# Decoder trunk: low parts of the input projections' weights and the rotary products on VectorE in place of GpSimd

## Chip, cores and metric

One core of one Trainium2 chip runs the whole program. The metric is the device time of one launch in microseconds (us). The kernel before took 2459.29 us, the median of three runs (2451.73 to 2461.47).

## What is computed

Two layers of a hybrid decoder on 1024 tokens of width 1024, in float32. Each layer has a mixer and a ConvFFN, each between two RMSNorms and added to the residual:

```python
h = rms_norm(x, norm_mix_pre[l])
proj = h @ w_in[l]                       # 1024 -> 3072, twelve slices of 256 columns
(c_a, c_gate, sb_q, sb_k, sb_v, r_q, r_k, r_v, r_g, sc_b, sc_c, sc_h) = jnp.split(proj, 12, axis=-1)
y_conf = conformer_conv(c_a, c_gate, ...)                  # depthwise conv of 31 taps, LayerNorm, SiLU
y_sb = stick_breaking_attention(sb_q, sb_k, sb_v)          # cumulative sums over keys
y_ret = retention_mixer(r_q, r_k, r_v, r_g, ...)           # rotary(q), rotary(k), chunks of 128
y_sc = short_gated_conv(sc_b, sc_c, sc_h, ...)             # 3 taps
mix = jnp.concatenate([y_conf, y_sb, y_ret, y_sc], -1) @ w_out[l]
x = x + rms_norm(mix, norm_mix_post[l])
f = conv_ffn(rms_norm(x, norm_ffn_pre[l]), ffn_up[l], ffn_conv_w[l], ffn_down[l])
x = x + rms_norm(f, norm_ffn_post[l])
```

`rotary` gives `x1*cos - x2*sin` and `x2*cos + x1*sin` for the two halves of each head of 64.

## The kernel before

**Split products.** A float32 matrix product is made of three products in the format fp32r: each operand is split into a high part (a cast, on ScalarE) and a low part (operand minus high part), and high*high, high*low and low*high are summed in PSUM. For the activations the parts are the resident tiles `hH` and `hL`; for the weights of the input projection they are `wh` and `wl`, made by `load_weight` (L189 to L196): a DMA of 512 KB into `wr` (L191), the cast `wh` on ScalarE (L193) and the subtraction `wl = wr - wh` (L195) on an engine that the caller names. There is one buffer `wr` and there are two of `wh` and `wl`: the next DMA into `wr` waits for L195, and a cast L193 waits until the projection two earlier has ended on TensorE.

**Projections.** `project` (L216) makes one block of 128 columns of the input projection in 8 steps, each of six matmuls of 512 columns (L210). There are 24 blocks in a layer (`IN_ORDER`). The list `WPOOL` names those whose L195 runs on GpSimd: 21 of the 24; `UPOOL` does so for the first six blocks of the up projection, which run the same way: one of six. So 44 subtractions L195 are on GpSimd (POOL in the profile) and 16 on VectorE (DVE).

**Order of the work.** Between the steps of the projections TensorE does the work of the attention groups, at slots set by hand: `run_slot` is called after each step, and inside the region `tc.manual_schedule` TensorE's order is as written. The other engines' orders are set when the program is built, by a scheduler with priorities and estimated costs; each engine then works strictly in that order and waits at semaphores.
- Stick-breaking attention, per unit: scores on TensorE into one PSUM tile (L361 to L364), three ACTIVATEs on ScalarE (L371 to L373), on VectorE a combination (L375) and a scan along the keys (L379), which reads the scores and so frees their tile for the next unit; then ScalarE (L381), transposes (L396), their split on ScalarE and VectorE (L181, L182), products with the values (L409) and their sums (L416 to L418).
- Conformer convolution: 31 taps for each of two channel blocks, each tap one operation of VectorE over 1023 columns or less with two inputs from SBUF (L261). They have a low priority and fill VectorE's order.
- Rotary products, `rotate` (L428 to L441): ScalarE copies the projected tile to SBUF, four DMAs swap the halves (L436), then `c = ps * c` on VectorE (L437) and on GpSimd `sw = sw * s` (L438) and `c = c + sw` (L439); the sum is split by L181 and L182. This is done for keys and queries of two head pairs, so 4 times in a layer.
- Retention: products per chunk on TensorE (L465 to L467), a chain of states over the chunks on VectorE and ScalarE (L474 to L479), scores (L490 to L492), their mask (L494), and outputs (L510, L512) with their sums (L514 to L516). L328, L329 split the queries of the second attention head pair; L314 are the value tiles' transposes; L524 takes a mean off in the retention's norm.

**Elsewhere.** `boundary` (L235) adds the residual and normalizes (L247, L249, L167); L731 is the output projection. The ConvFFN (L894 the products, L919 to L948 their evictions, L786 to L795 convolution and gate) and the down projection (L966, L967 the split, L977 the products) use GpSimd for L967. The first two weights of layer 2's input projection are loaded at the end of layer 1's ConvFFN.

Of the kernel before, what the change touches and what calls it, by code (L numbers as in the profile page):

```python
# [67 lines left out]
OTHER = (0, 2, 4)  # L68
HPR = 1000
HPW = 0  # L70
WPOOL = [0,1]+list(range(5,24))
UPOOL = (1,)
SKEW = 0
NPLAIN = 3
HPE = 60
# [11 lines left out]
def trunk_kernel(ctx, tc, x, w_in, w_out, w_up, w_down, params, gains, consts, rope, out):  # L87
    nc = tc.nc
# [25 lines left out]
    def ualloc(dt=F32, shape=(P, T)):  # L114
        s = free.pop(0)
        count[0] += 1
        t = big.tile(list(shape), dt, tag=f"u{s}", name=f"u{s}_{count[0]}")
        slot_of[id(t)] = (s, t)
        return t
# [81 lines left out]
    def prefetch(n=1):  # L201
        while queue and len(ready) < n:
            with tc.high_priority(offset=HPW):
                ready.append(load_weight(*queue.pop(0)))
# [224 lines left out]
    def rotate(ps, cs, done):  # L429
        c, s = cs  # L430
        e = ualloc()
        nc.scalar.copy(e, ps)
        sw = ualloc()
        for b in range(4):
            o = b ^ 1
            nc.sync.dma_start(sw[32 * b:32 * b + 32], e[32 * o:32 * o + 32])  # L436
        nc.vector.tensor_mul(c, ps, c)  # L437
        nc.gpsimd.tensor_mul(sw, sw, s)  # L438
        nc.gpsimd.tensor_add(c, c, sw)  # L439
        done(e, sw, s)  # L440
        return c  # L441

# [102 lines left out]
    nc.scalar.preload_act_table_set("natural_log_exp_and_others")  # L545
    queue += [(w_in[0, n], nc.gpsimd if n in WPOOL else nc.vector) for n in range(24)]
    hhs = []
# [24 lines left out]
    for l in range(DEPTH):  # L572
# [44 lines left out]
        def evict(kind, i, ps, cs):  # L617
# [24 lines left out]
            elif kind == "sv":  # L642
# [5 lines left out]
                for u in st["units"]:  # L648
                    u.update(v=v2, y=y[2 + i])
            elif kind == "rk":  # L650
                st["rk"] = rotate(ps, cs, later)
            elif kind == "rq":
                st["rq"] = rotate(ps, cs, later)
            elif kind == "rv":
                rv = ualloc()
# [118 lines left out]
        gd = dr.tile([NF, P, T], F32, name=f"gd{l}")  # L774
        queue += [(w_up[l, n], nc.gpsimd if n in UPOOL else nc.vector) for n in range(2 * NPLAIN)]
        prefetch(2)
# [279 lines left out]
        for ci, ch in enumerate(chunks):  # L1056
            final = ci == len(chunks) - 1
            if final:
                if not last:
                    queue += [(w_in[l + 1, n], nc.gpsimd if n in WPOOL else nc.vector) for n in range(24)]  # L1060
                    prefetch(2)
# [92 lines left out]
```

## Time and profile before

| | |
|---|---|
| median of three runs | 2459.29 us (2451.73 to 2461.47) |
| the profiled execution | 2450.47 us, its span 2448.7 us |
| TensorE (PE) busy | 2335.7 us, 95% |
| VectorE (DVE) busy | 1630.6 us, 67% |
| ScalarE (ACT) busy | 1093.6 us, 45% |
| GpSimd (POOL) busy | 391.3 us, 16% |
| granted TensorE clock, mean | 0.983 |

Times in rows are us from the start of the span. The span has these stages: the first norms to 50, mixer of layer 1 to about 540, its ConvFFN to about 1240, mixer of layer 2 to about 1760, its ConvFFN to the end. "Busy" is the time between the recorded start and end of an engine's instructions, whatever they did in it; bracketed text behind a row is the idle time of the engine before it and what ended it. A granted clock of 1.00 is TensorE's level of 2.4 GHz, 0.50 that of 1.2 GHz.

### The profile page before, as it was taken

How to read it: one execution, taken by the hardware profiler on the slowest of the kernel's cores; microseconds unless marked ns; L12 is line 12 of the kernel's file. 1: busy time of each engine (PE TensorE's matmuls, PEld its weight loads, DVE VectorE, ACT ScalarE, POOL GpSimd, SP SyncE). 2: the span in 40 equal slices, each digit the busy share in tenths (PEclk: the TensorE clock that was granted, in tenths of full speed). 3: DMA queues.
4: the chain of work that ended last, by engine and by line, in shares of the span. 5: the costliest groups of instructions: out<-in, count | busy, mean ns of one | idle time of the engine just before them, and what ended most of it. 6: DMA issues, size and time to landing. Idle time of an engine off the chain costs nothing. (4 is left out here: it accounts for less than half of the span.)

```text
span 2448.7 us, 26417 instructions
## 1 busy us (share of the span) xinstructions
PE 2335.7 (95%) x10596; PEld 1905.8 (78%) x10596; DVE 1630.6 (67%) x1657; ACT 1093.6 (45%) x1479; POOL 391.3 (16%) x160
## 2 busy tenths in 40 slices
PE   7988999999999999899999889999999999989998
PEld 6866787777888887688778667877788888877887
DVE  5599665649687777444556995656497787763445
ACT  5652564434454545511246435644344454553202
POOL 1131120000000002743111312100000000045520
PEclk9998999999999999999999989999999999999999
DMA  4212112312222223423222122123122222224213
GB/s 146 69 43 61 52 44 78 124 73 79 69 78 87 94 78 136 158 82 115 74 82 78 44 60 61 35 72 135 61 86 86 78 78 86 95 103 172 86 69 121
DMA packets 58811, 209.88 MB, mean 86 GB/s; under 512 B 7104, under 2 KB 7872, under 8 KB 58688
## 3 DMA queue, kind: packets, MB, share of 16 engines
q1 hardware_dynamic: 58688, 208.19, 25.3%
q8 instruction: 83, 1.36, 0.2%
q14 instruction: 40, 0.33, 0.0%
HBM read 159.93 MB, written 39.85 MB: 82 GB/s over the span
## 5 line engine op out<-in xcount | busy, mean ns | idle before, releaser
L261 DVE SCALAR_TENSOR_TENSOR u<-u,par,u 128x1023 f32<-128x1023 f32 (+11 forms) x280 | 393.4, 1417 | 46.3 <-ACT u L786 41.3
L989 DVE TENSOR_TENSOR u<-u,pp 128x1024 f32<-128x1024 f32 x143 | 174.6, 1221 | 238.1 <-PE pp L977 238.0
L210 PE MATMUL pp<-hH,wh 128*128 128x512 f32 x960 | 326.9, 411 | 0.6 <-DVE u L182 0.6
L210 PE MATMUL pp<-hL,wh 128*128 128x512 f32 x960 | 312.4, 396 | 0.0
L210 PE MATMUL pp<-hH,wl 128*128 128x512 f32 x960 | 310.5, 394 | 0.0
L977 PE MATMUL pp<-u,u 128*128 128x512 f32 x1152 | 271.7, 396 | 16.7 <-ACT u L948 9.6
L967 POOL TENSOR_TENSOR u<-u,u 128x1024 fp32r<-128x1024 f32 x48 | 120.0, 2517 | 1039.1 <-DVE u L940 956.7
L977 PEld LDWEIGHTS pp<-u,u 128*128 128x128 f32 x1152 | 218.5, 191 | 66.8 <-ACT u L948 10.4
L195 POOL TENSOR_TENSOR wl<-wr,wh 128x1024 fp32r<-128x1024 f32 x44 | 111.0, 2522 | 742.4 <-ACT wh L193 742.2
L210 PEld LDWEIGHTS pp<-hL,wh 128*128 128x128 f32 x960 | 183.3, 191 | 40.3
L210 PEld LDWEIGHTS pp<-hH,wl 128*128 128x128 f32 x960 | 182.7, 190 | 40.2
L210 PEld LDWEIGHTS pp<-hH,wh 128*128 128x128 f32 x960 | 172.4, 192 | 36.4 <-issue 4.8
L731 PE MATMUL pp<-u,hH 128*128 128x512 f32 x512 | 140.6, 395 | 0.5 <-ACT u L181 0.4
L977 PE MATMUL pp<-hH 128*128 128x512 f32 x576 | 131.5, 389 | 0.0
L977 PEld LDWEIGHTS pp<-hH 128*128 128x128 f32 x576 | 108.1, 188 | 22.5
L894 PE MATMUL ppx<-u,wh 128*128 128x512 f32 x384 | 118.6, 390 | 1.8 <-ACT u L935 1.5
L786 ACT ACTIVATE u<-u,par 128x1024 f32<-128x1024 f32 x76 | 87.7, 1154 | 71.2 <-DVE u L940 65.7
L731 PEld LDWEIGHTS pp<-u,hH 128*128 128x128 f32 x512 | 95.8, 190 | 21.0 <-ACT u L181 1.4
L966 ACT CAST u<-u 128x1024 fp32r<-128x1024 f32 x48 | 50.1, 1050 | 138.2 <-DMA u<-in_w_down 87.2
L894 PE MATMUL ppx<-u,hH 128*128 128x512 f32 x352 | 108.5, 389 | 1.5 <-ACT u L919 1.5
L193 ACT CAST wh<-wr 128x1024 fp32r<-128x1024 f32 x60 | 63.0, 1049 | 95.5 <-PE pp L210 55.1
L182 DVE TENSOR_TENSOR u<-tp,u 128x512 fp32r<-128x512 f32 x96 | 62.4, 683 | 38.9 <-ACT u L181 38.6
(244 smaller groups left out, 4550.5 us busy)
## 6 DMA issues: line engine op xcount, KB each, us to landing
wr<-in_w_up SPq DMA_DIRECT2D x50, 512.0 KB, 3.5
wr<-in_w_in SPq DMA_DIRECT2D x48, 512.0 KB, 3.6
gd<-u SPq DMA_DIRECT2D x44, 512.0 KB, 2.9
u<-in_w_down SPq DMA_DIRECT2D x44, 512.0 KB, 4.8
u<-gd SPq DMA_DIRECT2D x44, 512.0 KB, 4.2
u<-in_w_up SPq DMA_DIRECT2D x38, 512.0 KB, 4.2
xs<-u SPq DMA_DIRECT2D x24, 512.0 KB, 2.6
u<-xs SPq DMA_DIRECT2D x24, 512.0 KB, 3.5
```

What stands on the lines that cost most here:

```text
L182: nc.vector.tensor_sub(l, src, h.bitcast(F32))
L193: nc.scalar.copy(wh, raw)
L195: eng.tensor_sub(wl, raw, wh.bitcast(F32))
L210: nc.tensor.matmul(ps[:, half * 512:(half + 1) * 512], w[:, kt, :], m[:, 4 * half:4 * half + 4, kt, :], start=(kt == 0 and m is hH and w i ...
L261: eng.scalar_tensor_tensor(acc[:, lo:hi], src[:, lo - s:hi - s], wc, acc[:, lo:hi], ALU.mult, ALU.add)
L731: nc.tensor.matmul(ps[:, hs], a[:, t, k, :], w[:, hs], start=(k == 0 and a is hH and w is wo[k][0]), stop=(k == KT - 1 and a is hL))
L786: nc.scalar.activation(acc, ps, AF.Copy, scale=par[:, w + 2:w + 3])
L894: nc.tensor.matmul(ps, a[:, kt, :], x(m, kt), start=start and kt == 0 and a is wh and m == 0, stop=kt == 3 and a is wl, skip_group_check=True)
L966: nc.scalar.copy(h, raw)
L967: (nc.gpsimd if n is not None or len(slot_of) % 2 else nc.vector).tensor_sub(lo, raw, h.bitcast(F32))
L977: nc.tensor.matmul(ps[:, hs], a[:, ts_], w[:, hs], start=(i == 0 and w is h and a is gh), stop=(i == len(gs) - 1 and a is gl))
L989: nc.vector.tensor_add(facc[t], facc[t], ps)
```

## The change

```diff
-WPOOL = [0,1]+list(range(5,24))
-UPOOL = (1,)
+WPOOL = []
+UPOOL = ()
...
         nc.vector.tensor_mul(c, ps, c)
-        nc.gpsimd.tensor_mul(sw, sw, s)
-        nc.gpsimd.tensor_add(c, c, sw)
+        nc.vector.tensor_mul(sw, sw, s)
+        nc.vector.tensor_add(c, c, sw)
```

All 60 subtractions L195 and the 16 operations L438 and L439 are then in VectorE's order; nothing of what is computed changes. On GpSimd 60 operations fewer are left (L967 and L247 stay). The scheduler sets VectorE's order anew. In the rows below `-` is a row of before only and `+` one of the change only.

On VectorE, layer 1, around the scan L379 of the tile `pp_23` (`u_49` and `u_54` are the accumulators of the two convolutions, `u_64` and `u_55` the rotated key's swapped and direct parts, `u_83` its low part):

```order
+L261 SCALAR_TENSOR_TENSOR u_49_842<-u_48_839,par,u_49_842 128x1011
+L438 TENSOR_TENSOR u_64_1108<-u_64_1108,u_56_979 128x1024
 L182 TENSOR_TENSOR u_71_1214<-tp,u_71_1214 128x4x128
 L182 TENSOR_TENSOR u_72_1222<-tp,u_72_1222 128x4x128
 L375 SCALAR_TENSOR_TENSOR u_70_1202<-pp_23_1189,u_69_1198 128x1024
-L182 TENSOR_TENSOR u_83_1464<-u_55_977,u_82_1463 128x1024
+L439 TENSOR_TENSOR u_55_977<-u_55_977,u_64_1108 128x1024
 L379 SCALAR_TENSOR_TENSOR u_70_1202<-pp_23_1189,u_70_1202 128x383
 L379 SCALAR_TENSOR_TENSOR u_70_1202<-pp_23_1189,u_70_1202 128x639
 L437 TENSOR_TENSOR u_67_1133<-pp_22_1137,u_67_1133 128x1024
+L195 TENSOR_TENSOR wl<-wr,wh 128x1024
 L417 TENSOR_TENSOR u_27_487<-op,u_27_487 64x2x128
```

The two rotary operations stand in front of the scan now, the split of the key behind it, and a weight's low part between the scan and the sums L417, L418.

On VectorE, layer 1, where the retention's chain of states begins (L474; a tap's last number tells how far the convolution is, from 1023 down to 994):

```order
-L261 SCALAR_TENSOR_TENSOR u_54_975<-u_53_971,par,u_54_975 128x1012
-L261 SCALAR_TENSOR_TENSOR u_54_975<-u_53_971,par,u_54_975 128x1011
-L261 SCALAR_TENSOR_TENSOR u_54_975<-u_53_971,par,u_54_975 128x1010
 L474 COPY acc_1546<-pp_28_1548 64x64 x2
 L476 SCALAR_TENSOR_TENSOR acc_1547<-acc_1546,gam,pp_28_1548 64x64 x2
-L261 SCALAR_TENSOR_TENSOR u_54_975<-u_53_971,par,u_54_975 128x1009
 L479 SCALAR_TENSOR_TENSOR u_90_1545<-acc_1546,gam,u_90_1545 128x64
+L261 SCALAR_TENSOR_TENSOR u_49_842<-u_48_839,par,u_49_842 128x997
```

Before, 44 taps stand ahead of L474 (the first accumulator is done to 994, the second to 1010). With the change 35 do (to 998 and to 1015); the nine others are later in the order.

On VectorE, layer 1, the first unit of the second attention head pair, as it was:

```order
L261 SCALAR_TENSOR_TENSOR u_54_975<-u_53_971,par,u_54_975 128x994
L516 TENSOR_TENSOR u_95_1653<-pp_34_1792,u_95_1653 64x512
L375 SCALAR_TENSOR_TENSOR u_105_1814<-pp_35_1804,u_104_1810 128x1024
L379 SCALAR_TENSOR_TENSOR u_105_1814<-pp_35_1804,u_105_1814 128x1023
L515 TENSOR_TENSOR u_95_1653<-pp_36_1839,u_95_1653 64x512
L516 TENSOR_TENSOR u_95_1653<-pp_36_1839,u_95_1653 64x512
```

The last tap is done ahead of this scan, and nothing stands between L375 and L379. The same place with the change:

```order
L375 SCALAR_TENSOR_TENSOR u_105_1814<-pp_35_1804,u_104_1810 128x1024
L195 TENSOR_TENSOR wl<-wr,wh 128x1024
L379 SCALAR_TENSOR_TENSOR u_105_1814<-pp_35_1804,u_105_1814 128x1023
L261 SCALAR_TENSOR_TENSOR u_54_975<-u_53_971,par,u_54_975 128x1002
L261 SCALAR_TENSOR_TENSOR u_54_975<-u_53_971,par,u_54_975 128x1001
L261 SCALAR_TENSOR_TENSOR u_54_975<-u_53_971,par,u_54_975 128x1000
L515 TENSOR_TENSOR u_95_1653<-pp_36_1839,u_95_1653 64x512
```

A weight's low part stands between L375 and the scan, and late taps behind the scan.

## Rows read from the trace of the kernel before

**Rows 1.** Page, busy time of the engines (us, share of the span, instructions).
```profile
PE 2335.7 (95%) x10596; PEld 1905.8 (78%) x10596; DVE 1630.6 (67%) x1657; ACT 1093.6 (45%) x1479; POOL 391.3 (16%) x160
```

**Rows 2.** Stretches: length; PE, PEld, DVE, ACT, POOL busy (count); clock, DMA share, GB/s.
```profile
113.60:216.70 103.10, 89.34 (x434) 72.71 (x434) 101.64 (x90) 51.04 (x63) 26.02 (x10) 0.97 0.15 47
...
252.90:290.00 37.10, 36.01 (x150) 26.87 (x150) 18.86 (x22) 20.21 (x25) 4.77 (x2) 0.90 0.17 53
...
1332.40:1435.50 103.10, 89.31 (x434) 72.64 (x434) 101.68 (x90) 50.99 (x63) 26.98 (x10) 0.97 0.16 46
...
223.10:233.10 10.00, 8.25 (x31) 7.58 (x32) 9.77 (x14) 1.90 (x6) 0.00 (x0) 0.50 0.34 79
250.40:260.40 10.00, 9.81 (x22) 6.89 (x23) 5.31 (x7) 3.72 (x4) 0.00 (x0) 0.50 0.00 0
```

**Rows 3.** What TensorE waited for, 113.6 to 265: total us, times, longest.
```profile
PE pp L361 <- DVE u L379: 8.0, 4, 2.9
PE pp L490 <- DVE u L182: 5.6, 1, 5.6
PE op L409 <- DVE u L182: 3.1, 2, 3.0
...
PE tp L314 <- DVE u L182: 1.6, 1, 1.6
```

**Rows 4.** Groups by line: busy us, mean ns; first 113.6 to 216.7, then all.
```profile
L261 DVE SCALAR_TENSOR_TENSOR u<-u,par,u 128x1023 f32<-128x1023 f32 (+29 forms) x44 | 66.1, 1536 | 0.9 <-ACT u L268 0.4
...
L261 DVE SCALAR_TENSOR_TENSOR u<-u,par,u x280: 1235/1279/3431, 113.7 to 2204.5; 128x1023 f32<-128x1023 f32 x82, 128x1021 f32<-128x1021 f32 x4, 128x1019 f32<-128x1019 f32 x4, 128x1017 f32<-128x1017 f32 x4
...
L195 POOL TENSOR_TENSOR wl<-wr,wh 128x1024 fp32r<-128x1024 f32 x44 | 111.0, 2522 | 742.4 <-ACT wh L193 742.2
...
L439 POOL TENSOR_TENSOR u<-u,u 128x1024 f32<-128x1024 f32 x8 | 21.7, 2717 | 0.6
...
L195 DVE TENSOR_TENSOR wl<-wr,wh 128x1024 fp32r<-128x1024 f32 x16 | 19.5, 1220 | 31.3 <-ACT wh L193 31.3
```

**Rows 5.** Order of time, POOL and DVE: start us, length us, instruction [idle before].
```profile
142.11 2.65 POOL L195 TENSOR_TENSOR wl<-wr,wh 128x1024 fp32r<-128x1024 f32 x1 [17.29 <-ACT wh L193]
...
142.40 3.43 DVE L261 SCALAR_TENSOR_TENSOR u<-u,par,u 128x1022 f32<-128x1022 f32 x1
...
162.80 3.14 DVE L182 TENSOR_TENSOR u<-u,u 128x1024 fp32r<-128x1024 f32 x1
```

**Rows 6.** Order of time, end of the chunk products and what follows.
```profile
210.70 0.28 PE L467 MATMUL pp<-u,u 128*128 128x128 f32 x1
...
216.64 0.21 DVE L474 COPY acc<-pp 64x64 f32<-64x64 f32 x1
...
235.86 1.04 ACT L193 CAST wh<-wr 128x1024 fp32r<-128x1024 f32 x1 [2.34 <-issue]
```

**Rows 7.** Order of time, the scan of the second pair's first unit.
```profile
260.09 1.23 DVE L375 SCALAR_TENSOR_TENSOR u<-pp,u 128x1024 f32<-128x1024 f32 x1 [2.17 <-ACT u L373]
261.35 2.35 DVE L379 TENSOR_TENSOR_SCAN u<-pp,u 128x1023 f32<-128x1023 f32 x1
...
262.38 1.05 ACT L193 CAST wh<-wr 128x1024 fp32r<-128x1024 f32 x1 [2.33 <-PE pp L210]
...
263.84 0.36 PE L510 MATMUL pp<-u,u 128*128 128x256 f32 x1 [1.09 <-DVE u L379]
```

**Rows 8.** Order of time, other places where a DVE instruction is long.
```profile
17.60 3.39 DVE L167 SCALAR_TENSOR_TENSOR u<-u,r,u 128x1024 f32<-128x1024 f32 x1
...
473.16 3.41 DVE L249 SCALAR_TENSOR_TENSOR u<-u,r,u 128x1024 f32<-128x1024 f32 x1 [2.56 <-ACT r L158]
...
473.10 2.39 POOL L195 TENSOR_TENSOR wl<-wr,wh 128x1024 fp32r<-128x1024 f32 x1 [61.75 <-ACT wh L193]
...
960.96 3.31 DVE L261 SCALAR_TENSOR_TENSOR u<-u,par,u 128x1022 f32<-128x1022 f32 x1
...
965.89 0.50 PE L894 MATMUL ppx<-u,hH 128*128 128x512 f32 x1 [1.48 <-ACT u L919]
```

## The prediction
> **What bounds the kernel now.** I read the page first. TensorE is busy for 95% of the span and VectorE for 67% [rows 1], so by the means TensorE is the bound and VectorE has room. The table of stretches says otherwise for one stage. From 113.6 to 216.7, where the first attention head pair, the convolutions and the rotary products meet, VectorE is busy for 101.64 of 103.10 us and TensorE for 89.34; layer 2 has the same stretch at 1332.4 with the same figures [rows 2]. So there TensorE idles 13.8 us in each layer, and the table of its waits says for what: for the scan L379 8.0 us, for the splits L182 ahead of L409 3.1 and of L314 1.6; behind the stretch another 5.6 for the split that L490 needs [rows 3]. All of it waits for VectorE. In this stage VectorE is the bound, and a microsecond taken from its work ahead of such a gate is worth about one.
>
> Then the question is what VectorE does with its 101.64 us. The groups show 44 taps L261 there, at 1536 ns, where the median of all 280 is 1279 and the longest 3431 [rows 4]. In order of time the reason shows: a tap that starts at 142.40, inside a subtraction on GpSimd from 142.11 to 144.76, takes 3.43 us and ends 1.07 after it; a split L182 at 162.80 takes 3.14 [rows 5], where an operation of that shape takes 1.22 [rows 4]. Such an operation, with both inputs in SBUF, stands still while GpSimd works and is then done; the trace books the wait as busy. So GpSimd's work is not free here: in the stretch it costs VectorE 44 x (1536 - 1279) ns = 11.3 us at the taps and 3.14 - 1.22 = 1.9 at that split, 13.2 in all.
>
> **The change part by part.**
>
> *The stretch ahead of L474, in both layers.* It gains the 13.2 us. It takes on five of the L195 and four of the rotary operations: 9 x 1.22 = 11.0 us. And nine taps leave it (44 to 35 in the second piece of the order), 9 x 1.28 = 11.5. Net: 13.2 + 11.5 - 11.0 = 13.7 us less ahead of L474. L474 is late now: its chunk products end at 210.98, it starts at 216.64 [rows 6], and the 5.6 us at L490 are this delay handed on. I don't take the whole 13.7. The first piece of the order shows two gates with added work ahead of them: L439 ahead of the scan, L195 ahead of L418. What stands behind them on ScalarE comes later by that, and VectorE meets it. I leave out two operations, 2.4 us: **-11.3 us a layer**. Bounds: -13.7, if no gate binds; 0, if what VectorE loses to GpSimd is time in which it would have waited anyway (its idle time there is 1.5 us, which speaks against that).
>
> *From L474 to the second pair.* One L195 stands there behind the chain's operations, on VectorE's way to the mask L494 and so to the outputs: **+1.2**. Bounds 0 and 1.2. Its weight is cast only at 235.86 [rows 6], so the DMA into `wr` that follows the subtraction, on SP now behind the copies L341 and L342 of the same place, is still in time.
>
> *The scan of the second pair's first unit.* Here the change adds a wait. L195 stands between L375 and L379 (third piece). The cast it needs starts at 262.38 and ends at 263.43, since it waits for a projection's end on TensorE; the scan started at 261.35 and TensorE's L510 already waited 1.09 us for it [rows 7]. Now the scan can't start before 263.43 + 1.22 = 264.65: **+3.3 a layer**. Bounds: 0, if TensorE ends that projection 3 us earlier against ScalarE's chain; +3.3, as both are tied to the same TensorE.
>
> *The nine late taps.* They go to 252.9 to 290, where VectorE is busy 18.86 of 37.10 us, so 18.2 are free against 11.5 + 1.2 [rows 2]. The idle time is in pieces of two to three us, though, and the last taps stand ahead of L524, which frees a PSUM tile. I take one tap: **+1.3**. Bounds 0 and all nine, 11.5.
>
> *The other added operations* (the rest of 60 x 1.22 = 73 us, on an engine that is idle for a third of the span): 290 to the end of the mixer, and 50 to 110. There their casts end shortly before VectorE comes, or it was idle; I take 0. Their cover is that idle time; a late split there would cost TensorE what it costs now in the dense stretch.
>
> *L249 behind the output projection*, in both layers: it takes 3.41 us beside the L195 on GpSimd that starts at 473.10 [rows 8]. On VectorE that L195 ends at 474.32 and L249 1.28 later, at 475.6 in place of 476.57; TensorE waits for what follows: **-1.0 a layer**, bounds 0 and -1.0.
>
> *Layer 1 to layer 2*, once: a tap at 960.96 takes 3.31 us beside an L195 on GpSimd; ScalarE's next evictions queue behind it and TensorE waits 1.48 us [rows 8]. The operation itself costs VectorE 1.22 behind that tap. **-2.0**, bounds 0 and -3.5 (1.48 + 3.31 - 1.28). *The start*, once: L167 takes 3.39 at 17.60 [rows 8]; two subtractions of 1.22 replace two such waits of 2.1: **-1.0**, bounds 0 and -2.1.
>
> Sum: 2 x (-11.3 + 1.2 + 3.3 + 1.3 - 1.0) - 2.0 - 1.0 = **-16 us**, 0.65%. The profiled execution took 2450.47 us, 8.8 less than the median of the three; against it the sum gives 2434.5, on the median's scale 2459.3 - 16 = **2443**.
>
> A rule speaks against the change. On VectorE the moved subtraction takes 1.22 us, on GpSimd 2.52 [rows 4], and VectorE is the engine without idle time in the stretch. The Trainium skill, Perfetto Trace Analysis, Optimizing Scalar/DVE Operations, says that with VectorE saturated it may pay to move work from it to GpSimd, and adds that the two share a read port, so that it might not. By its first half the stretch would grow by the 11.0 us of the nine operations; by its second half it would not gain from GpSimd's help; the 13.2 us above bear the second out, and the first is the third rival below.
>
> **The rivals.**
>
> *More is won: TensorE's clock.* From 223.1 to 233.1 and from 250.4 to 260.4 the granted clock is 0.50, the lower level, the first time after the wait of 5.6 us at L490. The first stretch ends in another wait for VectorE, so it costs little; in the second TensorE is busy 9.81 of 10 us [rows 2], and at the full level the same work would take half: 4.9 us. With a shorter wait ahead of it that stretch may keep its clock: 2 x 4.9 = 9.8 more, 2433, and with every bound of the sum (2 x 14.7 + 3.5 + 2.1 + 9.8 = 44.8) 2414. Against it: the longer wait at the scan in the same place.
>
> *It is given back.* VectorE reaches L474 earlier, but the wait at L195 and the late taps take it back in front of the second pair: +3.3 + 1.2 and, say, five taps, 6.4, against -11.3. With the other terms that is 2 x (-0.4 - 1.0) - 3 = -6: 2453, no change that a measurement can tell.
>
> *Slower: VectorE is the bound, and gets more.* If the 13.2 us don't come back, because operations with SBUF inputs are then held by something else in the stretch, it has 11.0 more and 11.5 less up to L474, -0.5; then +1.2 and +3.3, and the taps find no room: half of them, 5.8. That is +9.8 a layer and, with the small gains gone too, 2479. It decides once the late work of 12.7 us no longer fits the 18.2 us of idle time behind the stretch. For it: VectorE is full there. Against it: the long operations all lie beside an operation on GpSimd, and are long by what is left of it.
>
> That the change doesn't do what it says can be left out: the order shows every operation on VectorE.
>
> **How the numbers follow.** Forecast -16 (-5 to -22): 0.47. The clock too: 0.20. Given back: 0.20. Slower: 0.13. A measurement of this kernel can tell about 0.5%, 12 us. Faster by more than that: the clock's case and two thirds of the forecast's, 0.52; slower 0.13; the rest, 0.35, within. The range is from 2414 (all bounds of gain with the clock) to 2463 (given back, and somewhat more).
>
> **What would show it.** Right: from 113 to 217 the taps' mean falls to about 1.28 us and none is over 1.5; the wait of L490 falls from 5.6 us to under 4, and the scans' 8.0 to under 4; L249 takes 1.28. The wait of L510 for the scan L379 in the second pair rises from 1.1 to over 4, in both layers. Wrong: if the taps are still long beside nothing on GpSimd, if TensorE's waits in the stretch stay at 13 us with VectorE full, or if new waits behind 265 exceed 6 us a layer.

## The result, and the profile after

With the change the kernel takes 2419.97 us, the median of four runs (2414.67 to 2421.7), against 2455.51 us (2449.76 to 2461.47) for the kernel before on the same chip: a ratio of 0.9858, 95% interval 0.983 to 0.9886. That is 35.5 us faster. The forecast was 16 (5 to 22); the whole range reached down to 2414. A second measurement of the same change gave 2418.49 us, ratio 0.985 (0.9835 to 0.9865).

The two profiled executions are 29.7 us apart (spans of 2448.7 and 2419.0 us). The page of after, busy time of the engines, answers to [rows 1]:

```profile
PE 2329.3 (96%) x10596; PEld 1901.0 (79%) x10596; DVE 1652.4 (68%) x1717; ACT 1094.2 (45%) x1479; POOL 239.4 (10%) x100
```

VectorE has 60 instructions more than before, and yet only 21.8 us more of busy time: 60 times 1.22 would be 73. Span less TensorE's busy time is its idle time: 113.0 us before, 89.7 after. So 23.3 of the 29.7 us are waits that are gone; the other 6.4 are less busy time for the same 10596 matmuls. The mean granted clock rose with it, from 0.983 to 0.985.

The stretch that VectorE bounds begins 1.83 us earlier in layer 1 and ends at L474, which now starts at 201.21 (216.64 in [rows 6]). The table of stretches of after (columns as in [rows 2]) for this stretch in both layers, and for two stretches of half clock behind it:

```profile
111.80:201.20 89.40, 83.43 (x419) 68.76 (x419) 87.19 (x89) 50.37 (x61) 0.00 (x0) 0.98 0.16 48
1311.10:1400.00 88.90, 82.30 (x422) 68.02 (x421) 87.50 (x91) 50.25 (x62) 0.00 (x0) 1.00 0.16 48
249.40:256.20 6.80, 5.96 (x13) 4.08 (x14) 6.32 (x6) 1.63 (x2) 0.00 (x0) 0.50 0.41 133
1447.50:1461.10 13.60, 12.50 (x27) 8.22 (x28) 9.13 (x9) 2.21 (x3) 0.00 (x0) 0.50 0.33 102
```

103.1 us have become 89.4. VectorE is still full there (87.19 of 89.40), so it is still the bound of this stretch; it just has less to do. The groups of the same stretch (111.8 to 201.2, VectorE) show the taps at their plain price, beside the operations that came:

```profile
L261 DVE SCALAR_TENSOR_TENSOR u<-u,par,u 128x1023 f32<-128x1023 f32 (+25 forms) x35 | 43.1, 1267 | 0.7 <-ACT u L268 0.4
...
L195 DVE TENSOR_TENSOR wl<-wr,wh 128x1024 fp32r<-128x1024 f32 x5 | 6.1, 1215 | 0.0
...
L438 DVE TENSOR_TENSOR u<-u,u 128x1024 f32<-128x1024 f32 x2 | 2.4, 1214 | 0.0
L439 DVE TENSOR_TENSOR u<-u,u 128x1024 f32<-128x1024 f32 x2 | 2.4, 1202 | 0.0
```

TensorE's waits from 111 to 250, to be read against [rows 3]:

```profile
PE pp L361 <- DVE u L379: 3.3, 3, 1.7
PE pp L490 <- DVE u L182: 2.2, 1, 2.2
PE pp L510 <- DVE u L516: 2.2, 1, 2.2
PE tp L396 <- DVE u L418: 1.6, 1, 1.6
PE pp L510 <- DVE u L329: 1.1, 1, 1.1
PE tp L314 <- DVE u L182: 0.9, 1, 0.9
```

The scans' 8.0 us are 3.3, L490's 5.6 are 2.2, and the 3.1 for L409 are gone. The wait for L329 is new, and the one for L418 was 0.8. Most of what is given back stands behind them, at the scan of the second pair. Its order of time, which answers to [rows 7]:

```profile
244.27 1.23 DVE L375 SCALAR_TENSOR_TENSOR u<-pp,u 128x1024 f32<-128x1024 f32 x1 [0.99 <-ACT u L373]
245.53 1.05 ACT L193 CAST wh<-wr 128x1024 fp32r<-128x1024 f32 x1 [1.29 <-PE pp L210]
246.61 1.23 DVE L195 TENSOR_TENSOR wl<-wr,wh 128x1024 fp32r<-128x1024 f32 x1 [1.11 <-ACT wh L193]
247.75 2.34 DVE L379 TENSOR_TENSOR_SCAN u<-pp,u 128x1023 f32<-128x1023 f32 x1
...
250.24 0.76 PE L510 MATMUL pp<-u,u 128*128 128x256 f32 x2 [4.29 <-DVE u L379]
```

The scan now waits for L195, L195 for its cast, and the cast for TensorE: the wait of L510 is 4.29 us where it was 1.09.

Where the 29.7 us went is found from the same places of the work in the two traces. "Waits" and "busy" are the change of TensorE's idle and busy time between the two marks, where the table of stretches was read for both:

| stretch (times of before) | before | after | change | forecast |
|---|---|---|---|---|
| 0 to 113.63, the start | 113.63 | 111.80 | -1.83 | -1.0 |
| to 224.85, first L490 of layer 1 | 111.22 | 97.61 | -13.6 (waits -11.2, busy -2.4) | -11.3 |
| to 290.02, second pair | 65.17 | 70.17 | +5.0 (waits +3.9, busy +1.1) | +5.8 |
| to 957.22, with L249 | 667.20 | 663.30 | -3.9 (waits -2.1, busy -1.8) | -1.0 |
| to 1016.26, into the down projection | 59.04 | 51.49 | -7.55 (waits -5.2, busy -2.4) | -2.0 |
| to 1332.45 | 316.19 | 316.80 | +0.6 | 0 |
| to 1443.62, first L490 of layer 2 | 111.17 | 96.60 | -14.6 (waits -10.6, busy -3.9) | -11.3 |
| to 1509.92, second pair | 66.30 | 73.89 | +7.6 (waits +3.9, busy +3.7) | +5.8 |
| to the end | 938.75 | 937.34 | -1.4 | -1.0 |

Two rows were mis-sized most: the dense stretch, where all 13.7 us of the working came, and the passage from the ConvFFN to the down projection, at whose end layer 2's first weights are prepared. Before, with 201 matmuls in it, and after, with the same 201 (times, then columns as in [rows 2]):

```profile
957.22:1016.26 59.04, 50.05 (x201) 38.70 (x199) 30.66 (x15) 32.34 (x36) 40.92 (x16) 0.94 0.49 175
```

```profile
942.88:994.37 51.49, 47.65 (x201) 38.27 (x200) 25.42 (x16) 31.16 (x34) 34.70 (x13) 0.97 0.49 176
```

GpSimd has 16 operations before and 13 after (L967 is left), VectorE one instruction more and 5 us less of busy time.

### The profile page after: what moved, and what is told of

It is laid out like the page before. It is cut to its first block, busy times and chain, and to the rows that moved or that the text cites. A ratio compares the mean times of both kernels' runs of the same rounds, so it can differ in the third digit from the quotient of the medians.

```text
span 2419.0 us, 26348 instructions
## 1 busy us (share of the span) xinstructions
PE 2329.3 (96%) x10596; PEld 1901.0 (79%) x10596; DVE 1652.4 (68%) x1717; ACT 1094.2 (45%) x1479; POOL 239.4 (10%) x100
## 4 chain that ended last, share of the span: by engine, by line
PE 37%; DVE 7%; ACT 3%; DMA 2%; issue 1%; POOL 0%; DVEq 0%; SPq 0%; POOLq 0%; ACTq 0%
PE pp L210 10%; PE pp L977 9%; PE ppx L894 8%; PE ppy L894 4%; DVE u L261 2%; PE ppz L894 2%; PE pp L731 1%; DVE u L182 1%; ACT u L151 1%; PE op L409 1%; DVE u L379 1%; DVE u L167 1%; DMA u<-gd 0%; PE tp L396 0%; DMA wr<-in_w_out 0%
## 5 line engine op out<-in xcount | busy, mean ns | idle before, releaser
L261 DVE SCALAR_TENSOR_TENSOR u<-u,par,u 128x1023 f32<-128x1023 f32 (+10 forms) x280 | 363.8, 1310 | 45.2 <-ACT u L786 40.9
L967 POOL TENSOR_TENSOR u<-u,u 128x1024 fp32r<-128x1024 f32 x48 | 119.6, 2507 | 1937.9 <-DVE u L940 1853.0
L894 PE MATMUL ppx<-u,wh 128*128 128x512 f32 x384 | 118.7, 390 | 1.8 <-ACT u L935 1.5
L966 ACT CAST u<-u 128x1024 fp32r<-128x1024 f32 x48 | 50.2, 1052 | 136.7 <-DMA u<-in_w_down 87.8
L195 DVE TENSOR_TENSOR wl<-wr,wh 128x1024 fp32r<-128x1024 f32 x60 | 73.6, 1227 | 51.6 <-ACT wh L193 51.4
L894 PE MATMUL ppx<-u,hH 128*128 128x512 f32 x352 | 108.4, 389 | 0.0
L379 DVE TENSOR_TENSOR_SCAN u<-pp,u 128x1023 f32<-128x1023 f32 (+3 forms) x64 | 87.7, 1401 | 0.7
```

The source lines that it names most:

```text
L195: eng.tensor_sub(wl, raw, wh.bitcast(F32))
L261: eng.scalar_tensor_tensor(acc[:, lo:hi], src[:, lo - s:hi - s], wc, acc[:, lo:hi], ALU.mult, ALU.add)
L379: nc.vector.tensor_tensor_scan(rev, z[:, o + 1:e + 1][:, ::-1], rev, r[:, e:e + 1], ALU.add, ALU.add)
L894: nc.tensor.matmul(ps, a[:, kt, :], x(m, kt), start=start and kt == 0 and a is wh and m == 0, stop=kt == 3 and a is wl, skip_group_check=True)
L966: nc.scalar.copy(h, raw)
L967: (nc.gpsimd if n is not None or len(slot_of) % 2 else nc.vector).tensor_sub(lo, raw, h.bitcast(F32))
```

## The experiments

Each is the change with one edit, unless it says otherwise. The theory: VectorE's operations with two inputs in SBUF stand still beside GpSimd's, and the change takes GpSimd's away. The rivals: it is only the new order of VectorE (nine taps later), or only TensorE's clock.

**The two parts alone.** The rotary operations alone: `WPOOL` and `UPOOL` as before.

> Only the 16 rotary operations L438 and L439 move to VectorE; the weights' low parts L195 stay where they were before. Ahead of L474 VectorE's order now has 40 taps (44 before, 35 with the whole change). Theory (VectorE stands still beside GpSimd's operations, some 1.3 us for each): of the ten GpSimd operations in the stretch from 113.6 to 216.7 four go, which gives back about 5.3 us; 4 x 1.22 us of work come and 4 x 1.28 of taps leave, so about -5.5 us a layer and, without the wait at the scan of the second pair, little of it given back: -11 us in all, 2444 to 2446. Rival (each engine's work is independent; the gain is that GpSimd's slow 2.7 us operations no longer delay the weights): moving the rotary operations alone gains nothing, within 3 us of before.

2450.14 us, ratio 0.9977 (0.9965 to 0.9989): 6 us faster. The taps' mean from 113 to 217 is 1421 ns, between 1536 and 1267. The direction is the theory's, the size half of what it said. The traces show where: the stretch up to L490 gained 5.4 us in layer 1, as expected, and 3.2 in layer 2, but the second pair behind it took 7.1 and 8.4 back, where the theory had little. Of these, 5.5 and 4.9 are busy time, at a granted clock of 0.79 in place of 0.86; the wait for the scan of the second pair (1.09 before) is 2.75 us here too. The profiled execution, 2453.61 us, is one of the slower of its twelve, so the trace gives the places and the median the size.

The weights alone: L438 and L439 on GpSimd.

> Only the subtractions L195 move to VectorE; the rotary operations stay on GpSimd. Ahead of L474 39 taps. Theory (VectorE stands still beside GpSimd): six GpSimd operations leave the stretch, which gives back about 7.9 us, 5 x 1.22 come and 5 x 1.28 leave: -8 us a layer, then +5 a layer by the wait for L195 between L375 and L379, -2 a layer at L249, and all of what the change gained once, between the layers -7.7 and at the start -1.9: about -20 us, 2435 to 2440. With the run of the rotary operations alone the two parts add up to the change's 30 to 35 us. Rival (the two parts are one gain, the nine taps fewer ahead of L474): this gains nearly all of the change, 2422 to 2426.

2428.18 us, ratio 0.9895 (0.9878 to 0.9913): 28 us faster, more than the theory's 20 and less than the rival's gain. With the 6 us of the other part that is 34 of 35.5: by the medians the parts add up, and the weights are four fifths. The theory's 20 us are those of the traces: the spans are 19.6 us apart (2448.7 and 2429.1), the stretch up to L490 gained 8.3 and 7.9 us (expected 8 a layer), and the passage between the layers 7.55 (expected 7.7). Its terms came from a trace of before that was faster than the median, and this run's trace is the slowest of its five; that is why the medians are 28 us apart.

**Order or standing still.** GpSimd works again, and VectorE's order stays as it is (in the second run, but for a few neighbours outside the attention groups). First in small operations:

```diff
-        eng.tensor_sub(wl, raw, wh.bitcast(F32))
+        eng.tensor_sub(wl, raw, wh.bitcast(F32)); [nc.gpsimd.tensor_add(scr, p, p) for p in (wh[:, j:j + 2, :].bitcast(F32) for j in range(0, KT, 2))]
```

> The change with additional work that nothing uses: behind each subtraction L195 GpSimd adds a weight's high part wh to itself, in four operations of 256 columns, into a scratch tile that is never read. The order on TensorE, VectorE, ScalarE and SP is row for row that of the change. Theory (VectorE stands still beside GpSimd): taps beside these are again long, their mean from 113 to 217 over 1.5 us; at 1 to 1.3 us for each of 10 or so weights there the stretch is 9 to 13 us longer in each layer, L249 and the passage between the layers lose what they had gained: 2440 to 2450, nearly the whole gain gone. Rival (the gain is VectorE's order, the nine taps that are moved behind L474): no change, 2418 to 2424, taps at 1.28 us.

2441.04 us, ratio 0.9942 (0.9921 to 0.9964): some 20 us of the gain are gone with the same order, so the order alone does not make all of it. In the dense stretch, though, little is gone: up to L490 the traces give 3.1 and 4.2 us more than with the change, which had gained 13.6 and 14.6. And the sign of the mechanism was not what was expected. The taps' mean is only 1319 ns, and it is GpSimd that is held: in order of time, four operations of 613 ns each (their median) take 5.36 us between VectorE's,

```profile
174.53 5.36 POOL L195 TENSOR_TENSOR scr<-wh 128x256 f32<-128x256 f32 x4 [13.21 <-ACT wh L193]
...
175.63 1.23 DVE L195 TENSOR_TENSOR wl<-wr,wh 128x1024 fp32r<-128x1024 f32 x1
176.78 1.10 DVE L182 TENSOR_TENSOR u<-u,u 128x512 fp32r<-128x512 f32 x1
177.80 1.61 DVE L261 SCALAR_TENSOR_TENSOR u<-u,par,u 128x1008 f32<-128x1008 f32 x1
```

and a VectorE operation loses 0.3 to 0.4 us to each. In the whole span VectorE is busy 1671.6 us, 19.2 more than with the change.

Then in one operation of the size that was moved:

```diff
-        eng.tensor_sub(wl, raw, wh.bitcast(F32))
+        eng.tensor_sub(wl, raw, wh.bitcast(F32)); nc.gpsimd.tensor_sub(raw, raw, wh.bitcast(F32))
```

> The change with additional work that nothing uses, of the size that was moved: behind each subtraction L195 on VectorE GpSimd does the same subtraction once more, 128x1024 in one operation, back into wr, whose next DMA waits for it as it did before. VectorE's order is that of the change row for row up to the end of the attention groups and differs by a few neighbours at the output projection and the up projection. Theory (VectorE stands still beside GpSimd, and that is what the change removes): operations with two inputs in SBUF are up to 3.4 us long again; the taps' mean from 113 to 217 is over 1.45 us and VectorE is busy 30 to 40 us longer in the whole span than with the change; the gain is gone, and since VectorE does the moved work too the time is 2450 to 2465. Rival (what the 256 column operations took, 20 us, is all there is, and the rest of the gain is the order): 2438 to 2445.

2488.84 us, ratio to before 1.0147 (1.0125 to 1.0168): 36 us slower than before and 69 slower than the change. Its page:

```profile
PE 2353.8 (95%) x10596; PEld 1916.5 (77%) x10596; DVE 1695.3 (68%) x1717; ACT 1093.6 (44%) x1479; POOL 410.6 (16%) x160
```

VectorE is busy 42.9 us longer than with the change for the same 1717 instructions, and the taps' mean from 113 to 217 is 1442 ns (expected over 1450):

```profile
L261 DVE SCALAR_TENSOR_TENSOR u<-u,par,u 128x1023 f32<-128x1023 f32 (+26 forms) x36 | 50.7, 1442 | 0.7 <-ACT u L268 0.4
```

The dense stretch decides, since VectorE's order is the same in it. The change, then this run, in layer 1 up to L490 (columns as in [rows 2]):

```profile
111.89:209.41 97.52, 89.34 (x444) 73.38 (x443) 94.86 (x109) 55.08 (x70) 0.00 (x0) 0.98 0.18 50
```

```profile
114.30:221.11 106.81, 92.17 (x444) 75.81 (x443) 103.81 (x110) 55.64 (x71) 16.44 (x5) 0.95 0.17 49
```

VectorE is busy 9.0 us longer with the same order, and 9.3 of the 13.6 us are gone with five operations on GpSimd, where before had ten; in layer 2, 10.7 of 14.6. The rival, 20 us and the rest from the order, falls.

In the whole span TensorE has 45.4 us more of idle and 24.5 more of busy time. The time is 24 us over the theory's range, though, and not all of it is standing still: `wr` is kept until GpSimd is done, and one wait of TensorE ahead of the up projection's products (L894 for L261) is 14.6 us where the change has 5.7. How the rest divides was not tried.

**The passage between the layers.** The first two weights of layer 2 on GpSimd:

```diff
-queue += [(w_in[l + 1, n], nc.gpsimd if n in WPOOL else nc.vector) for n in range(24)]
+queue += [(w_in[l + 1, n], nc.gpsimd if n < 2 else nc.vector) for n in range(24)]
```

> The change as it is, but the first two weights of layer 2's input projection have their subtraction L195 on GpSimd again. VectorE's order differs by these two operations alone. Theory: the passage from layer 1 to layer 2 lost 7.7 us in the trace with the change, because the two operations on GpSimd held VectorE and also stood ahead of L967 on GpSimd; all of it comes back, 2427 to 2429 (+7 to +8 over the change), with the gaps of TensorE between 957 and 1016 as before and nothing different elsewhere. Rival (the 7.7 us come from elsewhere: VectorE's order in the ConvFFN or a clock that happens to be granted longer): +3 us or less, the -2.0 of the prediction undone.

2423.19 us, ratio 0.9874 (0.9855 to 0.9892), 3 us over the change (expected 7 to 8). The median speaks for the rival, the trace for the theory. The passage with its 201 matmuls is nearly what it was before:

```profile
943.19:1001.38 58.19, 49.70 (x201) 38.76 (x199) 30.68 (x15) 32.36 (x36) 41.00 (x16) 0.94 0.49 175
```

58.19 us against 51.49: two subtractions on GpSimd cost 6.7 us here. The two runs with a part of the change agree: with the weights alone moved the passage takes 51.5 us, with the rotary operations alone 58.6. In the same trace layer 2 gave back 2.3 us less behind its L490 than in the change's first trace, since the half clock fell elsewhere, and the change's second trace does that too. How much of the 6.7 us the median keeps is open. TensorE's waits from 930 to 1016, of this run and then of the change:

```profile
PE pp L977 <- ACT u L948: 4.3, 1, 4.3
PE pp L977 <- ACT u L987: 2.5, 3, 1.4
PE ppx L894 <- ACT u L919: 1.5, 1, 1.5
...
```

```profile
PE pp L977 <- ACT u L948: 3.3, 1, 3.3
PE pp L977 <- ACT u L987: 0.5, 1, 0.5
PE ppx L894 <- ACT u L935: 0.4, 1, 0.4
```

The prediction knew the third line of this run alone. The other two are evictions on ScalarE that stand behind a cast L966, and the order of time of ScalarE in this run shows that cast waiting for GpSimd (in the whole passage the casts L966 wait 4.5 us for L967, with the change 1.5):

```profile
968.03 1.04 ACT L966 CAST u<-u 128x1024 fp32r<-128x1024 f32 x1 [1.43 <-POOL u L967]
968.99 1.15 ACT L786 ACTIVATE u<-u,par 128x1024 f32<-128x1024 f32 x1
970.04 0.56 ACT L948 COPY u<-ppx 128x512 f32<-128x512 f32 x1
```

The casts ahead of L987 wait for DMAs, whose buffers L967 gives back; that these come late for that reason is read from the code, not tried.

**The scan without the wait.** That one weight on GpSimd, `WPOOL = [15]`:

> The change, but of the 24 weights of a layer the one whose L195 stands between L375 and L379 of the second pair's first unit keeps it on GpSimd. Theory (the wait of 4.29 us of L510 for that scan, in each layer, is the wait of L195 for its cast, handed on): the wait falls to 1.5 us or less, some 3 us a layer come back, perhaps with the stretch at half clock behind it: 2411 to 2415. Rival (TensorE waits for ScalarE's chain there all the same, or the tap that now stands between L375 and L379, held by GpSimd's operation, takes 3 us): the wait stays over 3 us and the time is 2417 to 2422.

2419.38 us (2410.74 to 2421.43), ratio 0.9855 (0.9833 to 0.9877): no difference to the change that its runs can tell, and so the rival's time. The wait fell to 2.39 and 2.58 us, between the two theories, and the order of time says why:

```profile
241.68 1.23 DVE L375 SCALAR_TENSOR_TENSOR u<-pp,u 128x1024 f32<-128x1024 f32 x1 [0.98 <-ACT u L373]
242.82 1.25 DVE L261 SCALAR_TENSOR_TENSOR u<-u,par,u 128x1002 f32<-128x1002 f32 x1
...
243.99 2.34 DVE L379 TENSOR_TENSOR_SCAN u<-pp,u 128x1023 f32<-128x1023 f32 x1
...
246.48 0.47 PE L510 MATMUL pp<-u,u 128*128 128x256 f32 x2 [2.39 <-DVE u L379]
```

A late tap of 1.25 us took the place of L195; the 1.09 us of before and these 1.25 make nearly all of the 2.39.

**What is left on GpSimd.** Both L247 and L967 on VectorE, then each alone, and the first with the one weight ahead of the scan on GpSimd:

```diff
-(nc.vector if f is ps or g_pre is None else nc.gpsimd).tensor_mul(tt, f, g_post)
+nc.vector.tensor_mul(tt, f, g_post)
...
-(nc.gpsimd if n is not None or len(slot_of) % 2 else nc.vector).tensor_sub(lo, raw, h.bitcast(F32))
+nc.vector.tensor_sub(lo, raw, h.bitcast(F32))
```

> The change, and the last work of GpSimd on VectorE as well: the 88 subtractions L967 of the down projection's weights and activations and the 8 products L247. Theory (what GpSimd costs VectorE is worth more than what it takes off it wherever VectorE has idle time): in the passages from the ConvFFN to the down projection, at 957 and 2151 in the trace of the change, the wait of L977 for ScalarE's L948 (3.31 and 5.23 us), ScalarE's waits for L967 and the long taps there go; -3 to -8 us, 2412 to 2417. Rival (VectorE's strict order: 96 x 1.22 us more on it, where evictions and sums of the down projection queue behind subtractions that wait for their casts): no gain or up to 8 us slower, 2419 to 2428.

2392.99 us, ratio 0.9762 (0.9739 to 0.9785): 60 us faster than before, 25 to 27 faster than the two medians of the change, more than either theory said.

> The change, and only the eight products L247 at the end of layer 1 on VectorE; L967 stays on GpSimd. In the run without GpSimd the stretch from 1180 to 1240 was 8.2 us shorter than with the change. Theory: that is L247, 2.75 us each on GpSimd in the chain from the last sums to the next layer's first projection, and 1.22 on VectorE: -8 us there and nowhere else, 2411 to 2414. Rival: L967, whose last subtractions lie there too, made it: -2 us or less, 2417 to 2421.

2408.69 us, ratio 0.9812 (0.9797 to 0.9826): 10 us by L247 alone (against the 2418.49), where 8 were expected. From 1170 to 1240 the traces give 8.2 of them, as the theory said; the groups of the change and of this run there:

```profile
L247 POOL TENSOR_TENSOR u<-u,u 128x1024 f32<-128x1024 f32 x8 | 22.0, 2752 | 72.0 <-issue 48.8 <-DVE u L989 23.2
L167 DVE SCALAR_TENSOR_TENSOR u<-u,r,u 128x1024 f32<-128x1024 f32 x8 | 13.8, 1720 | 3.1 <-ACT r L158 3.0
```

```profile
L167 DVE SCALAR_TENSOR_TENSOR u<-u,r,u 128x1024 f32<-128x1024 f32 x8 | 10.2, 1279 | 0.7 <-ACT r L158 0.7
...
L247 DVE TENSOR_TENSOR u<-u,u 128x1024 f32<-128x1024 f32 x8 | 9.7, 1217 | 0.1
```

TensorE waited 7.6 us for L167 there with the change and not at all in this run. It is the same picture in small: the operation is faster on VectorE (1217 ns, not 2752), and its neighbour L167 is no longer held (1279, not 1720).

> The change, and only the 88 subtractions L967 on VectorE; L247 stays on GpSimd. Theory: this is the rest of what the run without GpSimd gained, in the passages at 957 and at 2151 to 2200 (there 8 and 3 us), -14 to -18 us: 2402 to 2406, and with the run of L247 alone it adds up to the 27 us. Rival: layer 2's clock happened to be better in that run, and L967 alone gives -5 us or less: 2414 to 2419.

2403.72 us, ratio 0.9792 (0.9778 to 0.9806): 15 us by L967 alone, the theory's size, and 10 and 15 make up the gain of both. Most of it is in one of the theory's two places. In layer 2, from the ConvFFN into the down projection, 10.7 us are gone (the change, then this run):

```profile
2110.03:2210.10 100.07, 89.96 (x384) 72.68 (x383) 51.95 (x41) 51.39 (x58) 50.24 (x20) 0.98 0.37 136
```

```profile
2102.86:2192.26 89.40, 87.12 (x385) 71.81 (x383) 65.34 (x62) 52.92 (x58) 0.00 (x0) 1.00 0.44 154
```

TensorE's idle time there fell from 10.1 to 2.3 us. But the passage of layer 1, the other place, takes 51.75 us, against 51.49 with the change: nothing came there. The rest of the 15 lies in stretches where the two traces of the change differ as well.

> The change, the last work of GpSimd on VectorE as in the run without GpSimd, and the one weight ahead of the scan on GpSimd as in the run with the free scan. If the two gains add up, 2405 to 2411, the fastest of all; if either is not there, its own time of that run's rival plus the other's gain, 2413 to 2420.

2396.34 us, ratio 0.9765 (0.9742 to 0.9787): the free scan adds nothing that its runs can tell here either, and both expected ranges were too slow, since they knew nothing of the 25 us. The fastest is the kernel with no work on GpSimd at all, 2393 us.

**The spread.** The change and the kernel before, once more each:

> The change itself once more, beside the three others. Theory: the two profiled executions compared so far were 29.7 us apart, the medians 35.5, because the one of before had a granted clock of 0.983, over the mean of its runs, 0.980; the change's median stays at 2419 to 2422 and a second trace of it has the same waits of TensorE to 0.2 us, other stretches at half clock and a span within 6 us of the first. Rival: the change's own time varies by more, or its median was low by chance with four runs: 2422 to 2428.

Its span was 2417.0 us, its median 2418.49, half a microsecond below the theory's range; the rival falls. The waits that the prediction is about are the same (4.29 at both scans, 2.20 and 2.21 at L490), but not all: L510 waited 3.5 us for L516 in layer 1, not 2.2.

> The kernel before once more, for a second trace of it. Theory: its runs differ by the granted clock (0.976 to 0.983 with 2449 to 2461 us): the waits of TensorE for VectorE are those of the first trace to 0.2 us, and a longer span, if there is one, comes with more or longer stretches at half clock. Rival: the waits themselves differ.

A miss. This execution was shorter, a span of 2444.1 us, and the waits of layer 1 were others: L490 waited 3.2 us, not 5.6, L314 3.0, not 1.6. Layer 2 had those of the first trace to 0.1 us. In layer 2 the half clock also came where it had come before, 41 and 75 us after the start of the dense stretch; in layer 1 it came at 25, 49 and 90 us, not at 41 and 75. That a drop of the clock at another place moves the waits for VectorE behind it fits this; it was not tried.

## Why the prediction was right or wrong

**The number: low.** 35.5 us are outside the forecast's own range of 5 to 22 and more than the clock's case gave (26). That the whole range held them is in part luck: its lower end was made of every bound of gain and of 9.8 us of clock, and the clock gave less, in other places. On the scale of the traces, 29.7 us against 16, most of the excess is in two terms, the stretch ahead of L474 and the passage between the layers; the other 6 us are the spread of the runs.

**The mechanism: right.** VectorE was the bound of the dense stretch and lost some 13 us there to GpSimd's work. With GpSimd silent the taps' mean is 1267 ns (forecast 1280), the longest of the 60 taps from 111.8 to 280 is 1285 ns. With whole operations on GpSimd again and VectorE's order the same in the stretch, taps are up to 3.4 us long and two thirds of its gain are gone.

**The stretch ahead of L474: mis-sized.** The working gave 13.7 us and I took 11.3, with 2.4 off for two gates that might bind. They did not: 103.1 us became 89.4, which is 13.7, and layer 2 gained 14.6 up to L490. The bound was the better estimate: VectorE, idle for 1.46 us in this stretch before, is idle for 2.21 in it now.

**The wait at the scan: right.** +3.2 us, forecast +3.3, in both layers, by the chain that was forecast (4.29 us at L510). With the late taps and the L195 at the mask the second pair lost 5.0 us in layer 1 (forecast 5.8) and 7.6 in layer 2. The waits are 3.9 in both; the rest is busy time, 1.1 and 3.7, with 6.8 and 13.6 us at half clock around this scan.

**Layer 1 to layer 2: the step that failed.** I took one long tap and one wait of 1.48 us there, -2.0 with a bound of -3.5; measured are -7.55, and 6.7 of it came back with the two operations on GpSimd alone. The term looked at VectorE only, and at one tap of it: VectorE is busy there for 5.2 us less, though one instruction more is on it. GpSimd has a queue of its own there, 16 operations in 59 us, busy for 40.92 of them; a cast on ScalarE waits for it, and TensorE waits for the evictions behind such casts. An operation that leaves that queue moves what stands behind it forward; how the 7.55 us divide between the two was not tried.

**L249 and the start: half the size.** TensorE's waits for L167 behind the output projection of layer 1 fell from 4.1 us (the longest 3.1) to 2.1 (1.2), forecast 1.0. L249 takes 1.28 us behind an L195, as I had charged:

```profile
460.30 1.23 DVE L195 TENSOR_TENSOR wl<-wr,wh 128x1024 fp32r<-128x1024 f32 x1 [2.33 <-ACT wh L193]
461.44 1.28 DVE L249 SCALAR_TENSOR_TENSOR u<-u,r,u 128x1024 f32<-128x1024 f32 x1
```

It ends 4.75 us after the L247 ahead of it, 5.97 before, which is 1.2 of the 2.0; what made the rest is open. The start gave 1.83, forecast 1.0; its bound was 2.1. Another 1.6 us between 290 and 957 are a stretch at half clock at 390.2 that is gone; the change's second trace has one at 378.8.

**The rivals.** *The clock too* came near in number, not in place: busy time fell by 6.4 us, forecast 9.8. But the half clock stayed at the second pair (249.4 and 1447.5 in the table of stretches), where busy time even rose; it fell ahead of L490, by 2.4 and 3.9 us, and between the layers, by 2.4. In which stretches the half clock falls differs between two traces of one kernel, so this part cannot be shared among the edits. The mean granted clock over 17 runs of before is 0.980, over the change's first four 0.985, and the profiled execution of before had 0.983; it took 2450.47 us, 5.0 less than the median of its round, and the change's 0.8 more than its own, which is why the medians are 35.5 us apart and the traces 29.7. Most of the other runs have no trace, so this last part is read from their clocks and times alone. *Given back* and *slower* did not come: behind the scan of the second pair TensorE waits for nothing new in layer 1's mixer beyond 0.2 us, and the late taps found room.

**The rule that spoke against the change.** The Trainium skill's page SBUF — State Buffer, in Who interferes with whom, says that an instruction of VectorE with two SBUF inputs contends with one of GpSimd that reads SBUF, and calls the pair of ports that the two share an exclusive lock. The runs agree for both sides: taps of 3.43 us beside whole subtractions on GpSimd, and GpSimd's operations of 613 ns that take up to 6.8 us between VectorE's. Operations with one input from PSUM stayed at their 1.2 us beside GpSimd, as the six L437 do that ran beside it before (1.19 to 1.22).

## What to carry to other kernels

Look for operations of one kind whose longest is more than twice their median, and lay the other engine's operations beside them in order of time: what an engine "takes over" may be paid for by the engine it was meant to relieve. Then a helper engine's price is its own time, plus what its neighbour stands still, plus what waits in its queue; here 60 operations of 2.5 us on GpSimd cost 35 us more than 60 of 1.22 on an engine that was already full in the stretch that counted. Where the profile shows such an engine at all, ask for every operation on it, not only for those in the busy stretch: the 96 that were left were worth another 25 us or so by the medians, 19 of them found in two places of the traces.

## What was not expected of the hardware

Who is held depends on how the work is cut. One GpSimd operation of 128x1024 with two inputs cost VectorE 0.72 us on average (42.9 us for 60); four of 128x256 that read one tile cost it 0.32 together (19.2 for 60), while GpSimd took 4.1 us for them (248 us for 60) in place of 2.4. And two runs of one kernel may differ by over 10 us: seventeen of the kernel before, taken together, lie between 2449.45 and 2461.21 us, with mean granted clocks between 0.976 and 0.983, and its two traces differ in their waits as well.
